# The down product of a SwiGLU network by seven block products in place of eight

## The chip, the cores and the metric

One core of a Trainium2 chip runs the whole encoder in one launch. The metric is device time in microseconds (us) of that launch. Five engines work side by side, each through its own instructions in program order: PE (TensorE: matmuls and transposes), ACT (ScalarE), DVE (VectorE), POOL (GpSimd) and SP, which only issues DMAs here. They wait for each other on semaphores.

## The reference, cut to what matters

256 tokens of width 1024 go through two layers. Each layer is: half an FFN, a token mixer, half an FFN. So there are four FFNs, all of this kind:

```python
def swiglu(h, w_gu, w_down):
    g, u = jnp.split(h @ w_gu, 2, axis=-1)
    return (jax.nn.silu(g) * u) @ w_down
# x = x + 0.5 * rms_norm(swiglu(rms_norm(x, g_pre), w_gu, w_down), g_post)
# h: 256 x 1024, w_gu: 1024 x 5632, w_down: 2816 x 1024, all float32
```

The first mixer is a retention layer, the second a latent attention. The change leaves both alone.

## The kernel before, in words

Every product of two float32 matrices is made of three matmuls in a rounded format: each operand is split into a high part (`h`, made by a cast on ACT) and a low part (`l`, the difference, made by a subtraction on DVE), and `mm3` (lines 135 to 138) adds high by high, high by low and low by high into one PSUM bank of 128 x 512. Weights go the same way: SP loads a raw tile, ACT casts it to `wh` (line 75), DVE subtracts to get `wl` (line 76). There are nine pairs of such weight tiles and five raw tiles, in rotation.

An FFN (`ffn`, from line 227) goes through 2816 inner columns in 11 chunks of 256. For chunk c and token half t (0 or 1), `gu(t, c)` makes the gate and up columns in one bank: 8 steps over the depth, 24 matmuls of 512 columns. `swiglu(t, c)` then reads the bank: a Silu on ACT (line 263), a multiplication on DVE (line 265), giving the activation `a`, and a block transpose on DVE (line 282) into `aT`. When two chunks and both halves are there, POOL and 12 small DMAs exchange blocks of `aT` into the tile `ag`, which holds the transposed activation (`turn`). `take(c)` splits it into `ah` and `al`; the table `landed` says behind which `swiglu` it is put: for an even chunk c behind `swiglu(0, c + 3)`, for an odd one behind `swiglu(1, c + 2)`. `both(c)` is the down product of a chunk: 2 token halves x 2 output halves x 2 depth blocks = 8 block products, 24 matmuls of 512 columns, summed over all chunks in four PSUM banks (`accs`). Four banks are left for gate and up.

PE's order is that of the Python code. In the main loop (c = 3 to 9) it is `gu(0, c)`, `gu(1, c)`, `both(c - 3)`. The order on ACT, DVE and SP is made by a scheduler when the kernel is built, from what is ready when in its own estimate and from edges such as `behind(s_ins, a_ins)`, which put one instruction behind another on the same engine. After that it is fixed. `post` scales a finished token half, adds it to `x` and prepares the next norm; the last call of it writes the output. The three Python functions at the end of the kernel (from line 1034) load `x` and the first weights and start the first FFN.

Of the kernel before, what the change touches and what calls it, by code (L numbers as in the profile page):

```python
# [18 lines left out]
P = 128  # L19
# [12 lines left out]
def kernel(ctx, tc, x, mem, positions, norm_gains, ffn_w_gu, ffn_w_down, w_o,  # L32
# [18 lines left out]
    def t2(name, n=512, dt=F32):  # L51
        return wk.tile([P, n], dt, name=name, tag="t2", bufs=8)
# [26 lines left out]
    def load_raw(src, cols):  # L79
        raw = raw_tile()  # L80
# [9 lines left out]
        return raw  # L90

    last_load = [None]

# [4 lines left out]
    ahead = []  # L98

# [43 lines left out]
    def rstd_of(halves, scale, eps, tag):  # L143
        ss = sm.tile([P, 2], F32, name="ss", tag="ss")
        for i, h in enumerate(halves):
            junk = wk.tile([P, 512], BF16, name="junk", tag="junk", bufs=1)
            S.activation(out=junk[:, :h.shape[1]], in_=h, func=AF.Square, scale=scale,  # L147
                         accum_out=ss[:, i:i + 1])
        ms = sm.tile([P, 1], F32, name="ms", tag="ms")
        if len(halves) == 2:  # L150
            V.scalar_tensor_tensor(out=ms, in0=ss[:, 0:1], scalar=eps, in1=ss[:, 1:2],
                                   op0=ALU.add, op1=ALU.add)
        else:
            V.tensor_scalar(out=ms, in0=ss[:, 0:1], scalar1=eps, scalar2=None, op0=ALU.add)
        r = sm.tile([P, 1], F32, name=tag, tag=tag)
        rsqrt(r, ms)
        return r
# [22 lines left out]
    def pre(t, gain):  # L180

        z = Z()
        parts = []
        for i in range(2):
            p = t2("z")
            V.tensor_tensor(out=p, in0=halves(xt[t])[i], in1=halves(gain)[i], op=ALU.mult)
            parts.append(p)

        def put_half(i):
            if i == 0:  # L190
                z.h, z.l = ztile()
# [5 lines left out]
        def put():  # L197
            put_half(0)
            with tc.issue_after(put_half(1)):
                rstd()  # L200
        z.put, z.put_half, z.rstd = put, put_half, rstd
        return z

    def post(t, accs, gain, half, next_gain, hook=None):
# [5 lines left out]
        ends = next_gain is None  # L210
        if not ends:
            scaled(0)
            scaled(1)
        r = rstd_of(accs, 1.0 / 16.0 if half else 1.0 / 32.0, (4.0 if half else 1.0) * EPS, "prs")
        if ends:
            scaled(0)
            scaled(1)
        for i in range(2):
            xx = halves(xt[t])[i]
            V.scalar_tensor_tensor(out=xx, in0=y[i], scalar=r, in1=xx, op0=ALU.mult, op1=ALU.add)  # L220
            if ends:
                nc.sync.dma_start(out=out[0, t * P:(t + 1) * P, i * 512:(i + 1) * 512], in_=xx)
            if hook and i == 0:
                hook()
        return None if next_gain is None else pre(t, next_gain)

# [5 lines left out]
    def ffn(l, j, zs, gains, extra=(), first=None):  # L232
        wgu, wd = ffn_w_gu[l, j], ffn_w_down[l, j]
        gu_w, d_w, act, at, pair = {}, {}, {}, {}, {}
        accs = [[None, None], [None, None]]
        extra = dict(extra)
# [7 lines left out]

        def gu(t, c, part=None):
            z = zs[t]
            if c not in gu_w:
                load_gu(c)
            if part != 1:
                act[t, c] = bank()  # L250
            p = act[t, c]
            for k in range(KB) if part is None else range(part * 4, part * 4 + 4):
                wh, wl = gu_w[c][k // 2]
                n = slice((k % 2) * 512, (k % 2 + 1) * 512)
                m = slice(k * P, (k + 1) * P)
                mm3(p, z.h[:, m], z.l[:, m], wh[:, n], wl[:, n], k == 0, k == KB - 1)
            if part is None:
                swiglu(t, c)

        def swiglu(t, c):  # L260
# [4 lines left out]
            a_ins = V.scalar_tensor_tensor(out=a, in0=p[:, FC:2 * FC], scalar=z.r, in1=s,  # L265
                                           op0=ALU.mult, op1=ALU.mult).ins
            if (t, c) == (1, NFC - 1) or first and (t, c) == (0, 0):
                ahead[:] = [s_ins, a_ins]
            act[t, c] = a
            if c < C:  # L270
                turn(t, c)
            for k in [k for k in list(pair) if landed(k) == (t, c)]:
                with behind(s_ins, a_ins):
                    take(k)

        def turn(t, c):
# [7 lines left out]
            if t == 1 and c % 2:  # L284
                g = wk.tile([P, 1024], F32, name="ag", tag="ag", bufs=1)
                for i in range(4):
                    sl = slice(i * 32, (i + 1) * 32)
                    G.tensor_copy(out=g[sl, i * 256:(i + 1) * 256], in_=b[sl, i * 256:(i + 1) * 256])  # L288
                    for q in range(4):
                        if q != i:  # L290
                            nc.sync.dma_start(out=g[q * 32:(q + 1) * 32, i * 256:(i + 1) * 256],  # L291
                                              in_=b[sl, q * 256:(q + 1) * 256])
                pair[c - 1], pair[c] = g, g
# [5 lines left out]
        def take(c):  # L299
            g = pair.pop(c)  # L300
# [14 lines left out]
        def down(t, c, hs=(0, 1)):  # L315
# [3 lines left out]
            for i in hs:  # L319
                if c == 0:  # L320
                    accs[t][i] = bank()
                for b in range(2):
# [4 lines left out]
                        c == 0 and b == 0, c == NFC - 1 and b == 1)  # L327

        def both(c):
            down(0, c)  # L330
            down(1, c)

        if first:
            gu_w[0] = first
            gu(0, 0, 0)
            zs[1].put()
            gu(0, 0, 1)
            swiglu(0, 0)
            gu(1, 0)
            gu(0, 1)  # L340
        else:
            gu(0, 0)
            gu(0, 1, 0)
# [4 lines left out]
        gu(1, 1)  # L348
        gu(0, 2)
        gu(1, 2)  # L350
        for c in range(3, C):
            gu(0, c)
            gu(1, c)
# [6 lines left out]
            both(c - 3)  # L360
# [8 lines left out]
        with in_order():  # L369
            z0 = post(0, accs[0], gain_post, True, next_gain, lambda: swiglu(1, C))  # L370
# [4 lines left out]
        if z0:  # L375
            z0.put()
        down(1, C, (1,))
        z1 = post(1, accs[1], gain_post, True, next_gain)
# [267 lines left out]
    def retention(zs, mkv, gains):  # L646
# [204 lines left out]
        z1 = post(1, W.accs[1], gain_post, False, next_gain)  # L851
        return [z0, z1]


    def mla(zs, mkv, gains):
# [173 lines left out]
        z1 = post(1, W.accs[1], gain_post, False, next_gain)  # L1029
        return [z0, z1]  # L1030
# [8 lines left out]
    g0 = wk.tile([P, DM], F32, name="gpre", tag="gpre", bufs=1)  # L1039
    grow = g0[0:1, 512:1024]  # L1040
    ones = k1("ones", P)[0:1, :]
    V.memset(ones, 1.0)
    nc.scalar.dma_start(out=grow, in_=norm_gains[0, 0, 512:1024].unsqueeze(0))
    load_x(0, 0)
    bcast(g0[:, 0:512], norm_gains[0, 0, 0:512])
    load_x(0, 1)
    first = [load_raw(gu_src(ffn_w_gu[0, 0], 0, u), 1024) for u in range(2)]
    for i in range(2):
        load_x(1, i)
    first += [load_raw(gu_src(ffn_w_gu[0, 0], 0, u), 1024) for u in range(2, 4)]  # L1050
# [10 lines left out]

    def warm(n):
        w = bank()
        for i in range(n):
            T.transpose(out=w[:, (i % 4) * P:(i % 4 + 1) * P], in_=ident, identity=ident)
    warm(8)
    g0 = [g0[:, 0:512], bank()]
    T.matmul(out=g0[1], lhsT=ones, rhs=grow, start=True, stop=True)
    with in_order():
        zs = [pre(0, g0)]  # L1070
        first[0] = split_raw(first[0], 1024, (lambda: zs[0].put_half(0), lambda: (warm(3), zs[0].put_half(1))))
        first[1] = split_raw(first[1], 1024, (lambda: None,) * 2)
        zs.append(pre(1, g0))
    zs[0].rstd()
    first[2:] = [split_raw(r, 1024) for r in first[2:]]
# [14 lines left out]
    def mem_extra(m):  # L1090
# [9 lines left out]
        return {6: first, 7: second, 8: third}  # L1100

    m0 = Mem(0)
    zs = ffn(0, 0, zs, lambda: (gpost(0, 1), gpre(0, 2)), {3: tables, 4: tables2, **mem_extra(m0)}, first=first)
    zs = retention(zs, m0, lambda: (gpost(0, 3), gpre(0, 4)))
    zs = ffn(0, 1, zs, lambda: (gpost(0, 5), gpre(1, 0)))
    m1 = Mem(1)
    zs = ffn(1, 0, zs, lambda: (gpost(1, 1), gpre(1, 2)), mem_extra(m1))
    zs = mla(zs, m1, lambda: (gpost(1, 3), gpre(1, 4)))
    ffn(1, 1, zs, lambda: (gpost(1, 5), None))
# [34 lines left out]
```

## Time and profile before

| what | value |
|---|---|
| device time, median of 3 runs (lowest, highest) | 964.87 us (963.84, 966.45) |
| the profiled execution's own time | 965.5 us |
| span of its trace, first to last instruction | 963.7 us |
| PE busy | 949.9 us, 99% |
| DVE busy | 626.2 us, 65% |
| ACT busy | 516.2 us, 54% |
| mean granted TensorE clock | 0.999 |

1.8 us of the profiled execution's time lie around the span. A busy PE is not a PE without slack: a matmul's record is longer than the step from one to the next, since they are pipelined, so the step has to be read from the start times. The idle time of ACT and DVE costs nothing as long as PE finds its operands.

### The profile page before, as it was taken

Reading aid. Unit: us, or ns where it says so; the run is one execution under the profiler, and the core shown is the slowest. Engines: PE = TensorE matmul, PEld = TensorE weight load, DVE = VectorE, ACT = ScalarE, POOL = GpSimd, SP = SyncE. Lnnn points to the kernel's source line nnn. Section 1 sums busy time; section 2 is a strip of 40 time slices with the busy share of each in tenths; the row PEclk is TensorE's granted clock in tenths of the full one; section 3 lists DMA queues with packets and bytes.
Section 4 is the critical chain, followed back from the end, with each engine's and each line's share of the span. In section 5 each row is a group of like instructions: output and inputs, shape, how many; then the busy total and the mean of one; then the engine's idle time right before and its main releaser. Section 6 shows DMA issues by size and latency. Waiting matters only on the chain.

```text
span 963.7 us, 13202 instructions
## 1 busy us (share of the span) xinstructions
PE 949.9 (99%) x4503; PEld 789.2 (82%) x4503; DVE 626.2 (65%) x989; ACT 516.2 (54%) x859; POOL 87.5 (9%) x122
## 2 busy tenths in 40 slices
PE   8999999999999999999999999999999999999997
PEld 6887888898878888888887888888897888888886
DVE  6766567586886775655558656655666886566552
ACT  6535456465665654544446444555568864444441
POOL 0110111010000111101101111101010011111010
PEclk9999999999999999999999999999999999999999
DMA  8668677493645556867546676875561746777631
GB/s 276 213 221 274 208 226 249 133 313 103 208 156 162 153 149 234 288 209 211 173 127 204 217 243 223 260 240 165 155 204 32 231 125 198 238 238 225 221 104 44
DMA packets 148679, 189.23 MB, mean 196 GB/s; under 512 B 13314, under 2 KB 130818, under 8 KB 148611
## 3 DMA queue, kind: packets, MB, share of 16 engines
q1 hardware_dynamic: 148608, 188.38, 61.2%
q8 instruction: 35, 0.57, 0.2%
q14 instruction: 34, 0.27, 0.1%
q10 hardware_dynamic: 2, 0.00, 0.0%
HBM read 179.42 MB, written 1.05 MB: 187 GB/s over the span
## 4 chain that ended last, share of the span: by engine, by line
PE 81%; DMA 7%; DVE 4%; ACT 3%; issue 3%; SPq 2%; POOL 0%; DVEq 0%; POOLq 0%; ACTq 0%
PE bank L138 26%; PE bank L136 26%; PE bank L137 26%; DMA raw<-in_ffn_w_gu_dram 4%; PE bank L162 2%; DVE wl L76 2%; ACT wh L75 2%; SPq L291 1%; DMA raw<-in_ret_w_in_dram 1%; DMA raw<-in_ffn_w_down_dram 1%; PE bank L493 1%; SPq L87 1%; ACT e L504 0%; DMA gpre<-in_norm_gains_dram 0%; DVE x L220 0%
## 5 line engine op out<-in xcount | busy, mean ns | idle before, releaser
L76 DVE TENSOR_TENSOR wl<-raw,wh 128x1024 fp32r<-128x1024 f32 (+2 forms) x326 | 388.6, 1209 | 164.6 <-ACT wh L75 158.2
L75 ACT CAST wh<-raw 128x1024 fp32r<-128x1024 f32 (+2 forms) x326 | 334.7, 1042 | 216.5 <-PE bank L138 78.4
L136 PE MATMUL bank<-wh,zh 128*128 128x512 f32 (+2 forms) x944 | 364.5, 386 | 0.6 <-ACT zh L75 0.4
L137 PE MATMUL bank<-wl,zh 128*128 128x512 f32 (+2 forms) x944 | 360.4, 382 | 0.6 <-DVE wl L76 0.6
L138 PE MATMUL bank<-wh,zl 128*128 128x512 f32 (+2 forms) x944 | 360.5, 382 | 0.4 <-DVE zl L76 0.4
L138 PEld LDWEIGHTS bank<-wh,zl 128*128 128x128 f32 x944 | 177.4, 188 | 35.4 <-DVE zl L76 1.4
L136 PEld LDWEIGHTS bank<-wh,zh 128*128 128x128 f32 x944 | 177.6, 188 | 34.8 <-ACT zh L75 0.9
L137 PEld LDWEIGHTS bank<-wl,zh 128*128 128x128 f32 x944 | 177.6, 188 | 34.5 <-DVE wl L76 1.6
L136 PE MATMUL bank<-wh,ah 128*128 128x512 f32 x352 | 138.0, 392 | 0.0
L138 PE MATMUL bank<-wh,al 128*128 128x512 f32 x352 | 137.4, 390 | 0.6 <-DVE al L76 0.6
L137 PE MATMUL bank<-wl,ah 128*128 128x512 f32 x352 | 137.0, 389 | 0.0
L288 POOL COPY ag<-aT 32x256 f32<-32x256 f32 x80 | 55.9, 699 | 481.6 <-DMA raw<-in_ffn_w_gu_dram 290.2
L263 ACT ACTIVATE s<-bank,rstd 128x256 f32<-128x256 f32 x88 | 41.5, 472 | 101.0 <-PE bank L138 100.9
L265 DVE SCALAR_TENSOR_TENSOR a<-bank,rstd,s 128x256 f32<-128x256 f32 x88 | 42.3, 480 | 59.5 <-ACT s L263 59.3
L138 PEld LDWEIGHTS bank<-wh,al 128*128 128x128 f32 x352 | 66.1, 188 | 15.2 <-DVE al L76 1.5
L137 PEld LDWEIGHTS bank<-wl,ah 128*128 128x128 f32 x352 | 66.1, 188 | 13.4
L136 PEld LDWEIGHTS bank<-wh,ah 128*128 128x128 f32 x352 | 66.1, 188 | 13.4 <-ACT ah L75 0.2
L147 ACT ACTIVATE junk<-bank 128x512 bf16<-128x512 f32 x24 | 14.3, 594 | 41.8 <-DVE y L209 29.4
L282 DVE STREAM_TRANSPOSE aT<-a 128x256 f32<-128x256 f32 x80 | 35.4, 443 | 1.5
L75 ACT CAST zh<-bank 128x512 fp32r<-128x512 f32 (+2 forms) x58 | 25.3, 462 | 19.4 <-PE bank L162 12.4
L76 DVE TENSOR_TENSOR zl<-bank,zh 128x512 fp32r<-128x512 f32 (+2 forms) x58 | 28.7, 519 | 6.0 <-ACT zh L75 6.0
L76 DVE TENSOR_TENSOR al<-ag,ah 128x256 fp32r<-128x256 f32 x80 | 31.3, 404 | 1.0 <-ACT ah L75 0.8
(154 smaller groups left out, 519.6 us busy)
## 6 DMA issues: line engine op xcount, KB each, us to landing
raw<-in_ffn_w_gu_dram SPq DMA_DIRECT2D x352, 256.0 KB, 4.7
raw<-in_ffn_w_down_dram SPq DMA_DIRECT2D x88, 512.0 KB, 5.4
raw<-in_ret_w_in_dram SPq DMA_DIRECT2D x48, 256.0 KB, 4.7
raw<-in_w_o_dram SPq DMA_DIRECT2D x16, 512.0 KB, 4.3
ag<-aT SPq DMA_DIRECT2D x240, 32.0 KB, 1.9
raw<-in_mem_w_kv_dram SPq DMA_DIRECT2D x8, 512.0 KB, 5.4
gpost<-in_norm_gains_dram SPq DMA_DIRECT2D x6, 512.0 KB, 6.2
gpre<-in_norm_gains_dram SPq DMA_DIRECT2D x5, 512.0 KB, 7.6
```

Of the source, the lines that this page charges most:

```text
L75: ins = S.copy(out=hi, in_=src).ins
L76: V.tensor_tensor(out=lo, in0=src, in1=hi.bitcast(F32), op=ALU.subtract)
L87: last_load[0] = nc.sync.dma_start(out=dst[:, k], in_=src[:, k]).ins
L136: T.matmul(out=dst, lhsT=ah, rhs=bh, start=start, stop=False)
L137: T.matmul(out=dst, lhsT=ah, rhs=bl, start=False, stop=False)
L138: T.matmul(out=dst, lhsT=al, rhs=bh, start=False, stop=stop)
L147: S.activation(out=junk[:, :h.shape[1]], in_=h, func=AF.Square, scale=scale, accum_out=ss[:, i:i + 1])
L162: T.transpose(out=tp[:s.shape[1], j * P:(j + 1) * P], in_=s, identity=ident)
L263: s_ins = S.activation(out=s, in_=p[:, 0:FC], func=AF.Silu, scale=z.r).ins
L265: a_ins = V.scalar_tensor_tensor(out=a, in0=p[:, FC:2 * FC], scalar=z.r, in1=s, op0=ALU.mult, op1=ALU.mult).ins
L282: V.transpose(out=b.rearrange("p (q u t b x) -> p u t q b x", q=4, u=2, t=2, b=2)[:, c % 2, t], in_=act.pop((t, c)).rearrange("p (b q x) - ...
L288: G.tensor_copy(out=g[sl, i * 256:(i + 1) * 256], in_=b[sl, i * 256:(i + 1) * 256])
```

## The change

In each FFN the down product of the first chunks (5 in the first and third FFN, 8 in the second and fourth; `fast`) is made by Strassen's scheme in its form with 15 additions. Token halves and depth blocks make a 2 x 2 block matrix of the activation, depth blocks and output halves one of the weights. Seven block products of 3 matmuls each (`down_fast`, 21 matmuls) take the place of eight. Their operands are sums and differences of blocks, made on DVE before the split: four of 128 columns for the activation (`take_fast`, tile `sr`), and three instructions of 1024, 512 and 512 columns for the weights (`load_fast`, tiles `wB` and `wB21`). The split parts get larger too: 3584 columns of weight in place of 2048 for a chunk, 896 of activation in place of 512.

The seven products are summed over the chunks in seven banks, and one bank is left for gate and up. So `swiglu` in these chunks copies the up half out of the bank on ACT before DVE multiplies. PE's order in the loop becomes `gu(0, c)`, 11 matmuls of `down_fast(c - 3)`, `gu(1, c)`, the other 10. `combine` adds the products up once, behind the last fast chunk, and the remaining chunks go on in four banks as before; `post` adds both sums.

Further edits come with it. The exchange into `ag` is cut into pieces of 2 (once 6) DMAs, each issued between two weight loads on SP. The take stands ahead of the transposes in `swiglu`. The first chunk of the first FFN is started by a class `First` that goes through the depth in 8 steps for both token halves. The tables and the memory loads move to other chunks, the square sum of `z0` at an FFN's end moves behind `post` of the other half, and the last output goes out in more pieces.

```diff
+        def load_fast(c):
+            w = wk.tile([P, 1536], F32, name="wB", tag="A", bufs=2)
+            w21 = esm("wB21")
+            with behind(*moved):
+                last_load[0] = nc.sync.dma_start(out=w[:, 0:1024], in_=block(c, 0, 0, 2)).ins
+            loaded()
+            with behind(*moved):
+                nc.sync.dma_start(out=w[:, 1024:1536], in_=block(c, 1, 1))
+                last_load[0] = nc.sync.dma_start(out=w21, in_=block(c, 1, 0)).ins
+            loaded()
...
+            split(three[:, 0:3:2], two(xh), two(xl))
+            V.tensor_tensor(out=w[:, 0:1024], in0=w[:, 512:1536], in1=w[:, 0:1024], op=ALU.subtract)
+            split(w[:, 0:1024], yh, yl)
+            split(w21, vh[:, lo], vl[:, lo])
+            V.tensor_tensor(out=three[:, 2], in0=three[:, 2], in1=three[:, 0], op=ALU.subtract)
+            split(three[:, 2], th, tl)
+            V.tensor_tensor(out=w21, in0=w21, in1=three[:, 2], op=ALU.subtract)
+            split(w21, vh[:, hi], vl[:, hi])
...
+        def take_fast(c):
...
+            V.tensor_tensor(out=q(sr, 0), in0=A[1][0], in1=A[1][1], op=ALU.add)
+            V.tensor_tensor(out=q(sr, 1), in0=q(sr, 0), in1=A[0][0], op=ALU.subtract)
+            V.tensor_tensor(out=q(sr, 2), in0=A[0][0], in1=A[1][0], op=ALU.subtract)
+            V.tensor_tensor(out=q(sr, 3), in0=A[0][1], in1=q(sr, 1), op=ALU.subtract)
...
+            split(A[1][1], q(ah, 2), q(al, 2))
+            split(sr, sh, sl)
...
+            at[c] = [a(0), z(3), z(0), z(2), a(1), a(2), z(1)]
+        def down_fast(c, *ms):
...
+            for m in ms:
+                p, x = divmod(m, 3)
+                (ah, al), (bh, bl) = at[c][p], d_w[c][p]
+                own = p in (1, 4, 5)
+                T.matmul(out=prod[p], lhsT=al if x == 2 else ah, rhs=bl if x == 1 else bh,
+                         start=c == 0 and x == 0, stop=x == 2 and c == fast - 1 and not own)
...
+            if 3 <= c < fast + 3 and (t, c) != (1, C):
+                u = k1("u")
+                s_ins = S.activation(out=u, in_=p[:, FC:2 * FC], func=AF.Copy, scale=z.r).ins
+                a_ins = V.tensor_tensor(out=a, in0=u, in1=s, op=ALU.mult).ins
...
-            if c < C:
-                turn(t, c)
             for k in [k for k in list(pair) if landed(k) == (t, c)]:
                 with behind(s_ins, a_ins):
                     take(k)
+            if c < C:
+                turn(t, c)
...
         for c in range(3, C):
             gu(0, c)
+            if c - 3 < fast:
+                down_fast(c - 3, *range(11))
             gu(1, c)
...
-            both(c - 3)
+            if c - 3 < fast:
+                down_fast(c - 3, *range(11, 21))
+                if c - 3 == fast - 1:
+                    combine()
+            else:
+                both(c - 3)
```

What this does to the order of the instructions is shown at three places. The first is PE in the second FFN, chunk 5. Names: `zh` and `zl` are the normed input, `ah`, `al`, `sh`, `sl` the split activation and its sums for chunk 2; `bank_3912` in the kernel before is the gate and up bank of token half 1. Before:

```order
L138 MATMUL bank_3876<-wh_3872,zl_3205 128x512
L136 MATMUL bank_3912<-wh_3851,zh_3354 128x512
...
L138 MATMUL bank_3912<-wh_3872,zl_3355 128x512
L136 MATMUL bank_3691<-wh_3967,ah_3906 128x512
L137 MATMUL bank_3691<-wl_3968,ah_3906 128x512
L138 MATMUL bank_3691<-wh_3967,al_3907 128x512
```

The same place now, with `bank_4086` and `bank_4170` as the gate and up banks of the two halves:

```order
L159 MATMUL bank_4086<-wh_4082,zl_3364 128x512
L367 MATMUL bank_3822<-wh_4138,ah_4117 128x512
L367 MATMUL bank_3822<-wl_4139,ah_4117 128x512
L367 MATMUL bank_3822<-wh_4138,al_4118 128x512
L367 MATMUL bank_3823<-wh_4138,sh_4120 128x512
L367 MATMUL bank_3823<-wl_4139,sh_4120 128x512
L367 MATMUL bank_3823<-wh_4138,sl_4121 128x512
L367 MATMUL bank_3824<-wh_4140,sh_4120 128x512
...
L367 MATMUL bank_3825<-wl_4141,sh_4120 128x512
L157 MATMUL bank_4170<-wh_4055,zh_3513 128x512
```

The 24 matmuls of token half 1 stood between the end of `gu(0, 5)` and the first matmul that reads `ah`. Now that matmul is the next one. The second place is ACT there now, from the Silu of `gu(0, 5)` (`s_4111`) on; `wB` and `wB21` are raw down weights, `raw` raw gate and up weights of the next chunk:

```order
L402 ACTIVATE s_4111<-bank_4086,rstd_3386 128x256
L406 ACTIVATE u_4114<-bank_4086,rstd_3386 128x256
L75 CAST wh_4140<-wB_4133 128x1024
L75 CAST ah_4117<-ag_3887 128x256
L75 CAST ah_4117<-ag_3887 128x128
L75 CAST wh_4142<-wB21_4134 128x512
L75 CAST wh_4235<-raw_4232 128x1024
L75 CAST sh_4120<-sr_4119 128x512
```

Before, the Silu was followed by the two casts to `ah` at once. The third place is DVE now in the chunk after it (6), from the last instructions ahead of the multiplication `a_4287` of `gu(0, 6)` on; `wl_4305` is the low part of the second group of down weights, which products 2 and 3 read:

```order
L76 TENSOR_TENSOR sl_4205<-sr_4203,sh_4204 128x512
L76 TENSOR_TENSOR wl_4303<-wB_4293,wh_4302 128x1024
L407 TENSOR_TENSOR a_4287<-u_4288,s_4285 128x256
L322 TENSOR_TENSOR wB_4293<-wB_4293 128x1024
L426 STREAM_TRANSPOSE aT_4291<-a_4287 128x4x64
L325 TENSOR_TENSOR wB_4293<-wB_4293 128x512
L76 TENSOR_TENSOR wl_4305<-wB_4293,wh_4304 128x1024
```

The difference of weights (line 322) and the low part made from it stand behind the multiplication that waits for `gu(0, 6)`. The kernel before had no such difference.

## Rows read from the trace of the kernel before

**Rows 1.** The page, sections 1 and 2: busy time of each engine, granted TensorE clock
```profile
PE 949.9 (99%) x4503; PEld 789.2 (82%) x4503; DVE 626.2 (65%) x989; ACT 516.2 (54%) x859; POOL 87.5 (9%) x122
...
PEclk9999999999999999999999999999999999999999
```

**Rows 2.** Waits of PE: waited for, us in total, times, longest
```profile
PE bank L162 <- DVE z L186: 2.5, 2, 1.3
PE bank L525 <- ACT pT L516: 1.4, 2, 0.9
```

**Rows 3.** Groups of PE by form: xcount, busy us, mean ns, idle before
```profile
L136 PE MATMUL bank<-wh,zh 128*128 128x512 f32 x864 | 340.7, 394 | 0.6 <-ACT zh L75 0.4
L136 PE MATMUL bank<-wh,ah 128*128 128x512 f32 x352 | 138.0, 392 | 0.0
```

**Rows 4.** Timeline of PE in the third FFN: start, duration, engine, line
```profile
649.03 0.39 PE L138 MATMUL bank<-wh,zl 128*128 128x512 f32 x1
649.26 0.39 PE L136 MATMUL bank<-wh,zh 128*128 128x512 f32 x1
...
654.48 0.39 PE L138 MATMUL bank<-wh,zl 128*128 128x512 f32 x1
654.70 0.39 PE L136 MATMUL bank<-wh,ah 128*128 128x512 f32 x1
```

**Rows 5.** Timeline of ACT in the same stretch
```profile
649.46 0.47 ACT L263 ACTIVATE s<-bank,rstd 128x256 f32<-128x256 f32 x1 [4.12 <-PE bank L138]
649.83 0.70 ACT L75 CAST ah<-ag 128x256 fp32r<-128x256 f32 x2
```

**Rows 6.** Timeline of DVE in the same stretch
```profile
649.97 0.48 DVE L265 SCALAR_TENSOR_TENSOR a<-bank,rstd,s 128x256 f32<-128x256 f32 x1 [2.34 <-ACT s L263]
650.37 0.42 DVE L76 TENSOR_TENSOR al<-ag,ah 128x256 fp32r<-128x256 f32 x1
650.70 0.44 DVE L282 STREAM_TRANSPOSE aT<-a 128x256 f32<-128x256 f32 x1
651.06 0.39 DVE L76 TENSOR_TENSOR al<-ag,ah 128x256 fp32r<-128x256 f32 x1
```

**Rows 7.** Groups of ACT by form: casts of 1024, 512 and 128 columns
```profile
L75 ACT CAST wh<-raw 128x1024 fp32r<-128x1024 f32 x314 | 326.4, 1054 | 211.9 <-PE bank L138 76.8 <-DMA raw<-in_ffn_w_gu_dram 58.4 <-DMA raw<-in_ffn_w_down_dram 48.6
...
L75 ACT CAST zh<-bank 128x128 fp32r<-128x128 f32 x20 | 5.7, 287 | 6.9 <-PE bank L525 4.2 <-DVE zl L76 2.7
...
L75 ACT CAST wh<-raw 128x512 fp32r<-128x512 f32 x4 | 2.3, 622 | 0.0
```

**Rows 8.** Groups of DVE by form: 1024 and 512 columns, and small ones
```profile
L76 DVE TENSOR_TENSOR wl<-raw,wh 128x1024 fp32r<-128x1024 f32 x314 | 379.2, 1224 | 162.9 <-ACT wh L75 156.5
...
L76 DVE TENSOR_TENSOR wl<-raw,wh 128x512 fp32r<-128x512 f32 x4 | 2.6, 683 | 0.0
...
L640 DVE TENSOR_TENSOR qs<-qs,krt 128x96 f32<-128x96 f32 x4 | 1.0, 257 | 0.0
```

**Rows 9.** The page, DMA issues: count, KB each, median us from issue to landing
```profile
raw<-in_ffn_w_gu_dram SPq DMA_DIRECT2D x352, 256.0 KB, 4.7
raw<-in_ffn_w_down_dram SPq DMA_DIRECT2D x88, 512.0 KB, 5.4
...
ag<-aT SPq DMA_DIRECT2D x240, 32.0 KB, 1.9
```

**Rows 10.** Timeline of PE at the start: first gate-and-up product to the third
```profile
9.00 0.72 PE L136 MATMUL bank<-wh,zh 128*128 128x512 f32 x1
...
22.98 0.39 PE L136 MATMUL bank<-wh,zh 128*128 128x512 f32 x1
```

**Rows 11.** Timeline of the end: last matmul and last scaling
```profile
957.24 0.39 PE L138 MATMUL bank<-wh,al 128*128 128x512 f32 x1
...
958.52 0.69 DVE L209 TENSOR_TENSOR y<-bank,gpost 128x512 f32<-128x512 f32 x1
```

More of the change, by code (lines that the diff above doesn't have):

```diff
@@ L98, with norm_behind @@
     ahead = []
+    behind_post = []
+    def norm_behind(z):
+        if z:
+            with behind(*behind_post):
+                z.rstd()
     def behind(*inss):
@@ L195, in rstd, with put, post @@
             z.r = rstd_of(halves(xt[t]), 1.0 / 32.0, EPS, "rstd")
-        def put():
+        def put(norm=True):
             put_half(0)
-            with tc.issue_after(put_half(1)):
-                rstd()
+            last = put_half(1)
+            if norm:
+                with tc.issue_after(last):
+                    rstd()
         z.put, z.put_half, z.rstd = put, put_half, rstd
         return z
-    def post(t, accs, gain, half, next_gain, hook=None):
+    def post(t, accs, gain, half, next_gain, hook=None, sums=(None, None)):
         y = [t2("y") for i in range(2)]
@@ L210, in post @@
         ends = next_gain is None
+        if sums[0] is not None:
+            for a, b in zip(accs, sums):
+                V.tensor_tensor(out=b, in0=a, in1=b, op=ALU.add)
+            accs = sums
         if not ends:
@@ L230, in gu_src, with ffn @@
                 .rearrange("(k p) (h f) -> p k h f", p=P, h=2)[:, :, :, c * FC:(c + 1) * FC])
-    def ffn(l, j, zs, gains, extra=(), first=None):
+    def ffn(l, j, zs, gains, extra=(), first=None, fast=0):
         wgu, wd = ffn_w_gu[l, j], ffn_w_down[l, j]
@@ new lines, in down_fast @@
+        def down_fast(c, *ms):
+            if c not in d_w:
+                load_fast(c)
+            if c == 0 and 0 in ms:
+                prod.extend(bank() for _ in range(7))
+                accs[0][:] = prod[4], prod[1]
+                accs[1][0] = prod[5]
+            for m in ms:
[4 more added lines that the diff above has]
+                         start=c == 0 and x == 0, stop=x == 2 and c == fast - 1 and not own)
@@ L245, in gu, with combine @@
+        def combine():
+            m1, m5, m7, m6 = prod[0], prod[2], prod[3], prod[6]
+            c1, u, v, w = esm("c1"), esm("u"), esm("v"), esm("w")
+            S.copy(out=c1, in_=m1)
+            add = lambda o, a, b: V.tensor_tensor(out=o, in0=a, in1=b, op=ALU.add)
+            add(u, m6, c1)
+            add(v, m5, u)
+            add(u, m7, u)
+            add(w, m5, u)
+            sums[:] = [[c1, v], [u, w]]
         def gu(t, c, part=None):
-            z = zs[t]
             if c not in gu_w:
@@ L285, in turn @@
                 g = wk.tile([P, 1024], F32, name="ag", tag="ag", bufs=1)
[L286 to L292, printed above, removed]
+                skip, n = (6, 6) if c == 1 else (4, 2) if c < C - 1 else (0, 12)
+                exchange(b, g, skip, n)
                 pair[c - 1], pair[c] = g, g
@@ L299, in take @@
         def take(c):
+            assert not between, between
+            if c < fast:
+                return take_fast(c)
             g = pair.pop(c)
@@ L333, in ffn @@
         if first:
[L334 to L339, printed above, removed]
+            gu_w[0] = first.w
+            first.run(lambda t, k: gu_k(t, 0, k))
+            load_gu(1)
+            for t in range(2):
+                first.rstd(t)
+                swiglu(t, 0)
             gu(0, 1)
@@ L1059, in gpost @@
         return gain_tile(norm_gains[l, j], "gpost")
+    wbank = bank()
     def warm(n):
-        w = bank()
         for i in range(n):
-            T.transpose(out=w[:, (i % 4) * P:(i % 4 + 1) * P], in_=ident, identity=ident)
+            T.transpose(out=wbank[:, (i % 4) * P:(i % 4 + 1) * P], in_=ident, identity=ident)
     warm(8)
[L1067 to L1073, printed above, removed]
```

232 lines of the change are left out of this document (187 added, 45 removed).

## The prediction

> **What bounds the kernel now.** I read the page first: PE is busy 99% of the span, DVE 65%, ACT 54%, and the granted clock is at its upper level (2.4 GHz) in all 40 slices [rows 1]. Then the waits of PE alone: the largest are 2.5 and 1.4 us in all [rows 2]. So nearly nothing is gained by making another engine faster, and nearly everything that makes PE wait shows in the time. Next, what a matmul costs. Its record is about 390 ns long [rows 3], but the timeline of PE shows 24 of them from 649.26 to 654.70 us [rows 4]: 5.44 / 24 = 0.227 us from one to the next. That step, not the 390 ns, is what a removed matmul gives back. Last, the same place on ACT and DVE, since it shows how long the answer to a gate and up product takes: the last matmul of it starts at 649.03, the Silu at 649.46, the next ACT instruction at 649.83; DVE multiplies from 649.97 to 650.45 [rows 4 to 6]. PE reads the new `ah` only at 654.70, since 24 other matmuls lie between. This is the cover that hides the answer now.
>
> **What is removed.** Three matmuls in each of 5 + 8 + 5 + 8 = 26 chunks: 78 x 0.227 = 17.7 us. The weight load of each is inside the step. Nothing on PE is added.
>
> **What is added on DVE and ACT.** For a chunk, DVE splits 1536 more weight columns (1.5 x 1.22 = 1.8 us), makes differences of 1024, 512 and 512 columns (1.22 + 2 x 0.68 = 2.6), four sums of 128 columns (no row of that size; 0.26 by the row of 96 columns; bounds 0.15 and 0.42, the latter for 256 columns; so 1.0) and splits 384 more columns of activation (0.4) [rows 6, 8]. Together 5.8 us. Before, 65% of the 16.3 us of a chunk (72 matmuls x 0.227) is 10.6 us, so now 16.4 us, against 69 x 0.227 = 15.7 us of PE. Even if nobody ever waited, DVE could not deliver the chunk in PE's time. ACT gets 1.6 us more of casts and two copies and stays below.
>
> **The wait at even chunks.** The loop now puts the first 11 matmuls of the down product straight behind `gu(0, c)`. The take of an even chunk is still placed behind `swiglu(0, c)` of that same product, on ACT as on DVE. So PE waits for an answer that it has only just made possible. I walk along the order shown for chunk 5, with time 0 at the start of the last gate and up matmul. ACT: Silu at 0.43, copy at 0.80, both done at 1.27 (the copy taken as long as the Silu); then in its order a cast of 1024 (done at 2.2), `ah` (0.35 and 0.29, done at 2.9), 512 (3.5), 1024 (4.5), `sh` 512 (5.15) [rows 5, 7]. DVE: the multiplication from 1.27 (0.40 to the next), three sums (2.45), transposes (0.36), the fourth sum (3.1), a low part of 1024 (4.3), `al` (0.33 and 0.26, 4.9), a low part of 512 (5.6), `sl` (6.2) [rows 6, 8]. PE's sixth matmul of the block reads `sl`. It could have started at 6 x 0.227 = 1.36, so it is 4.9 us late, and with it all that is queued behind it on PE: five more matmuls, `gu(1, c)`, the rest. ACT and DVE go on with weights in that time, so the later parts of the block find theirs. For chunk 0 of an FFN the order has one long instruction less on each engine: 4.2 us. For chunks 4 and 6 the second group of weights is made earlier: 3.7 us. There are 4 chunks 0, 4 chunks 2, 4 chunks 4 and 2 chunks 6: 4 x 4.2 + 4 x 4.9 + 6 x 3.7 = 58.6 us. Bounds: if nothing foreign stood between, the chain copy, multiplication, four sums, cast `sh`, `sl` would end at 1.27 + 0.40 + 1.04 + 0.62 + 0.68 = 4.0, 2.7 us late, 38 us for 14 chunks; with one more 1024-column instruction ahead of each (1.22), 76 us.
>
> **The wait at odd chunks.** Their take stands behind `swiglu(1, c)` a chunk earlier and has 34 matmuls of cover. But on DVE the difference of weights that products 2 and 3 need stands behind the multiplication of `gu(0, c)`. From time 0 again: multiplication done at 1.67, difference 1.22 (2.9), its cast on ACT 1.05 (3.9), its low part 1.22 (5.2) [rows 6 to 8]. PE's eighth matmul reads it and was due at 1.82: 3.3 us. Besides, SP has the second load of these weights behind the first piece of the exchange, which waits for the transposes of `gu(1, c)`. These end about 3.7 us behind its last matmul (copy, multiplication, four sums, `al`, transposes), and `gu(0)` of the next chunk ends 34 x 0.227 = 7.7 us behind it. The first cast of the chunk (1.05) needs that load and stands ahead of the Silu, so the load has 7.7 + 0.43 - 1.05 - 3.7 = 3.4 us to land unnoticed. It has 256 KB; loads of 32 KB land in 1.9 us, of 512 KB in 5.4 [rows 9]. So 0 to 2.0 us; I take 1.0. That is 4.3 us at 10 chunks (1 and 3 in the short ones, 1, 3 and 5 in the long ones; chunk 7's order has the difference ahead): 43 us, with bounds 33 and 53.
>
> **The rest.** At the start, the two halves of chunk 0 take PE from 9.00 to 22.98 us [rows 10], where 48 matmuls need 10.9; in 8 steps for both halves at once some of the 3 us of gaps go. A gain of 0 to 5 us, I take 3. At the end one addition of 512 columns from PSUM comes between the last matmul and the square: 0.69 by the scaling of that form [rows 11]; inside, three FFN ends cost 0 to 1.4 each, I take 0, since the other token half's matmuls cover them. `combine` gives DVE 4 x 0.69 us per FFN, 0 to 2.8; I take 0, hidden by the weights made ahead. The one bank for gate and up must be read within 10 or 11 matmuls (2.3 to 2.5 us) and is free at 1.27: no cost, up to 0.4 us if a 1024-column cast stands ahead. Moved tables and memory loads: PE does not wait for them before and has more time now; nothing.
>
> **The sum**, against the profiled execution: 965.5 - 17.7 + 58.6 + 43 - 3 + 0.7 = 1047 us; the median of the runs is 0.6 lower, so 1046. With the bounds of the two waits and of the start: 965 - 17.7 + 38 + 33 - 5 = 1013 and 965 - 17.7 + 76 + 53 + 3 = 1079.
>
> **Rivals.** *Only the bare chain counts.* The order of ACT and DVE is fixed, but if both run ahead during the waits, the odd chunks lose nothing and the even ones the 2.7 us: 965 - 17.7 + 38 - 3 = 982. For it speaks that DVE is idle a third of the time now; against it, that the difference stands behind the multiplication in every odd chunk named. 0.12.
>
> *PE's clock falls in the waits.* The trace shows no waits of this length in the stream of matmuls and the upper level throughout, so it cannot tell. If the granted clock fell to 1.2 GHz for the 11 matmuls behind each of the 24 waits, each would take a step twice as long: 24 x 11 x 0.227 = 60 us more, 1106. 0.10. The Trainium skill says, in "TensorE: Matmul & The Clock Gate" under "HAM oscillation", that pauses for other work between bursts of matmuls put the clock back and that each burst then starts slow. By that rule the time would be near this rival's; the trace neither agrees nor differs.
>
> *Faster, or the same.* If PE found its operands after all, because the answer takes less than the walk says, DVE would set the pace at about 16.4 us per chunk or somewhat below, against 16.3 before: between nothing and the whole 17.7 us, so 946 to 963, say 955. It decides at a wait of 2 x 3 x 0.227 = 1.36 us per pair of chunks: below that the change gains. For it speaks that this kernel hides such answers everywhere (the largest sums of waits are 2.5 and 1.4 us [rows 2]); against it, that the first read of `ah` follows its own product directly, and that Silu and copy alone put it 1.27 us behind. 0.09.
>
> **How the numbers follow.** The forecast has 0.69, the others 0.12, 0.10 and 0.09. A measurement of this kernel can tell a difference of 0.3% (2.9 us) from none. Of the last rival 0.07 is faster and 0.02 the same; 0.01 of the first is the same too. So faster 0.07, same 0.03, slower 0.90. The range goes from 990, between the bare chain and the lower bound, to 1090, between the upper bound and the clock rival's time; that leaves out about 0.2.
>
> **What would show it.** PE's waits by name: in the timeline of a chunk with even number a gap of 2 us or more behind the last gate and up matmul, ended by the cast to `ah`, and one ended by `sl`; in odd chunks one ended by the cast and low part of the difference of weights. PE's busy time lower by some 18 us and its idle time higher by 100. A pair of fast chunks should take about 39 to 40 us in place of 32.7. I am wrong if these gaps stay under 1 us, if DVE is busy 95% in these stretches with PE waiting for gate and up weights, or if the granted clock falls.

## The result, and the profile after

The changed kernel takes 1086.52 us (median of 4 runs, 1082.06 to 1087.57) against 964.91 (963.84 to 966.45): a ratio of 1.125 [1.123, 1.127]. It is slower, as forecast, and 40 us above the predicted 1046. It lies inside the stated range of 990 to 1090, but above 1079, where the sum of the waits ends with all its upper bounds. The profiled execution took 1087.57 us with a span of 1085.8, so 1.8 us lie around the span, as before.

The page after, sections 1 and 2, against [rows 1]:

```profile
PE 990.6 (91%) x4425; PEld 796.4 (73%) x4425; DVE 785.2 (72%) x1318; ACT 590.1 (54%) x1031; POOL 80.8 (7%) x122
...
PEclk9988899999999989988999898999999998989999
```

There are 78 matmuls fewer (4503 to 4425), yet PE's busy time rose by 41 us, and the granted clock is no longer at 9 in all slices; its mean is 0.953 (1.0 is the upper level, 2.4 GHz, and 0.5 the lower, 1.2 GHz). So part of the new time is idle PE, part is slower PE. The waits of PE, where [rows 2] had nothing above 2.5 us (waited for: us in total, times, longest):

```profile
PE bank L367 <- ACT ah L75: 46.4, 14, 7.2
PE bank L367 <- ACT wh L75: 18.8, 20, 1.5
PE bank L367 <- DVE wl L76: 14.6, 20, 0.8
PE bank L367 <- DVE al L76: 3.0, 6, 0.8
...
PE bank L367 <- DVE sl L76: 0.9, 3, 0.3
```

All lie in the first 11 matmuls of a fast chunk (line 367): 14 waits for `ah`, at the even chunks, and 20 each for `wh` and `wl`, two of each at the 10 odd chunks.

An even chunk, the place that the prediction walked along (second FFN, `gu(0, 5)` and the down product of chunk 2), in the timeline of all engines (start, duration, engine, line):

```profile
435.51 0.39 PE L159 MATMUL bank<-wh,zl 128*128 128x512 f32 x1
435.94 0.47 ACT L402 ACTIVATE s<-bank,rstd 128x256 f32<-128x256 f32 x1 [1.05 <-PE bank L159]
436.18 1.22 DVE L322 TENSOR_TENSOR wB<-wB 128x1024 f32<-128x1024 f32 x1
436.31 0.47 ACT L406 ACTIVATE u<-bank,rstd 128x256 f32<-128x256 f32 x1
437.32 0.42 DVE L407 TENSOR_TENSOR a<-u,s 128x256 f32<-128x256 f32 x1
437.44 1.04 ACT L75 CAST wh<-wB 128x1024 fp32r<-128x1024 f32 x1 [0.66 <-DVE wB L322]
...
438.39 0.60 ACT L75 CAST ah<-ag 128x256 fp32r<-128x256 f32 x2
...
438.84 0.50 PE L367 MATMUL bank<-wh,ah 128*128 128x512 f32 x1 [2.94 <-ACT ah L75]
...
440.40 0.80 PE L367 MATMUL bank<-wh,al 128*128 128x512 f32 x1 [0.82 <-DVE al L76]
...
441.03 0.80 PE L367 MATMUL bank<-wh,sh 128*128 128x512 f32 x1
441.07 0.68 DVE L76 TENSOR_TENSOR sl<-sr,sh 128x512 fp32r<-128x512 f32 x1
441.63 0.63 PE L367 MATMUL bank<-wl,sh 128*128 128x512 f32 x1
...
442.05 0.63 PE L367 MATMUL bank<-wh,sl 128*128 128x512 f32 x1
```

Time 0 is 435.51. The Silu comes at 0.43 as in [rows 5], the multiplication at 1.8, the cast to `ah` at 2.9, and the sixth matmul, which reads `sl`, at 6.5; the walk said 0.43, 1.3, 2.2, 6.2. The multiplication is late because DVE is in a difference of weights (line 322) from 436.18. After the first gap the matmuls also step differently: 441.63 to 442.05 is 0.42 us, where [rows 4] have 0.227. That is 1.85 times as long, and the granted clock there is 0.50, the 1.2 GHz level, in the last of these windows (us of the window, busy time of PE, PEld, DVE, ACT and POOL, granted clock, DMA share, GB/s):

```profile
436.00:439.00 3.00, 0.16 (x1) 0.16 (x2) 2.97 (x9) 2.34 (x6) 0.00 (x0) 1.00 1.02 346
439.00:442.00 3.00, 2.18 (x5) 1.13 (x6) 3.00 (x6) 2.93 (x4) 0.00 (x0) 0.72 0.21 83
442.00:446.00 4.00, 4.00 (x15) 3.24 (x15) 3.73 (x5) 2.29 (x4) 0.00 (x0) 0.78 0.02 4
446.00:450.00 4.00, 4.00 (x19) 3.30 (x19) 3.06 (x4) 0.97 (x2) 0.00 (x0) 1.00 0.00 0
441.00:443.00 2.00, 2.00 (x6) 1.51 (x6) 2.00 (x4) 1.17 (x2) 0.00 (x0) 0.50 0.04 8
```

The clock falls behind the gap of 2.94 us and is back at the upper level in the window from 446, with PE busy in between. DVE was done with `sl` at 441.75, 6.2 us from time 0 as the walk said; the slow step put its read 0.3 us behind that. The clock did not fall everywhere: by the trace's record of it, in or behind 18 of the 24 blocks, and of the four blocks whose only gap was 2.17 us behind two.

The odd chunk after it (`gu(0, 6)`, down product of chunk 3), same view:

```profile
457.13 1.05 ACT L75 CAST wh<-wB 128x1024 fp32r<-128x1024 f32 x1 [4.15 <-DMA wB<-in_ffn_w_down_dram]
457.16 0.39 PE L159 MATMUL bank<-wh,zl 128*128 128x512 f32 x1
...
459.35 0.42 DVE L407 TENSOR_TENSOR a<-u,s 128x256 f32<-128x256 f32 x1
...
459.69 1.22 DVE L322 TENSOR_TENSOR wB<-wB 128x1024 f32<-128x1024 f32 x1
...
460.94 1.57 ACT L75 CAST wh<-wB 128x1024 fp32r<-128x1024 f32 x2 [2.02 <-DVE wB L322]
...
462.01 1.82 DVE L76 TENSOR_TENSOR wl<-wB,wh 128x1024 fp32r<-128x1024 f32 x2 [0.18 <-ACT wh L75]
462.03 0.49 PE L367 MATMUL bank<-wh,sh 128*128 128x512 f32 x1 [1.10 <-ACT wh L75]
...
463.29 0.50 PE L367 MATMUL bank<-wl,sh 128*128 128x512 f32 x1 [0.77 <-DVE wl L76]
```

Cast late for its load, multiplication, difference (line 322), its cast, its low part, PE: the chain of the prediction, in its order. The eighth matmul comes at 463.29, due at 457.16 + 8 x 0.227 = 458.98, so 4.3 us late, as forecast. Why the load is late stands on SP (DMA queue):

```profile
435.49 0.55 SPq L309 DMA_DIRECT2D wB<-in_ffn_w_down_dram  x1
453.02 1.21 SPq L267 DMA_DIRECT2D ag<-aT  x2
454.27 0.58 SPq L312 DMA_DIRECT2D wB<-in_ffn_w_down_dram  x1
```

SP issues nothing from 436.0 to 453.0: the first piece of the exchange waits for the transpose of `gu(1, 5)`, and the second load of chunk 3's weights, with all loads behind it, waits in line. The sum of these waits in SP's queue:

```profile
SPq L267 <- DVE aT L426: 222.3, 18, 21.6
```

**Where the 122 us lie.** I added up, over all matmuls of 512 columns, what each step has above 0.227 us, apart for steps at a wait and steps without one. At waits: 4.4 us before, 100.2 after, so +95.8. Without a wait: 6.8 before, 52.4 after, so +45.6; steps at a granted clock below 1 have 42 us of it. The first such matmul starts at 6.42 in place of 9.00 [rows 10], -2.6:

```profile
6.42 0.67 PE L157 MATMUL bank<-wh,zh 128*128 128x512 f32 x1
```

The last one starts 7.5 us ahead of the span's end in place of 6.5 [rows 11], +1.1:

```profile
1078.26 0.39 PE L159 MATMUL bank<-wh,al 128*128 128x512 f32 x1
```

With the removed matmuls, -17.7, that makes 95.8 + 45.6 - 2.6 + 1.1 - 17.7 = 122.2, and the span grew by 1085.8 - 963.7 = 122.1.

### The profile page after: what moved, and what is told of

The parts are those of the page before. It is cut to its first block, busy times and chain, and to the rows that moved or that the text cites. A ratio compares the mean times of both kernels' runs of the same rounds, so it can differ in the third digit from the quotient of the medians.

```text
span 1085.8 us, 13518 instructions
## 1 busy us (share of the span) xinstructions
PE 990.6 (91%) x4425; PEld 796.4 (73%) x4425; DVE 785.2 (72%) x1318; ACT 590.1 (54%) x1031; POOL 80.8 (7%) x122
## 4 chain that ended last, share of the span: by engine, by line
PE 61%; DMA 11%; DVE 10%; SPq 10%; ACT 5%; issue 3%; POOL 0%; DVEq 0%; POOLq 0%; ACTq 0%
PE bank L157 16%; PE bank L158 16%; PE bank L159 16%; PE bank L367 7%; DMA raw<-in_ffn_w_gu_dram 5%; SPq L267 4%; SPq L91 3%; DVE wl L76 3%; DMA wB<-in_ffn_w_down_dram 3%; PE bank L187 2%; ACT wh L75 2%; DMA raw<-in_mem_norm_dram 1%; DMA raw<-in_ret_w_in_dram 1%; DVE a L407 1%; DVE al L76 1%
## 5 line engine op out<-in xcount | busy, mean ns | idle before, releaser
L76 DVE TENSOR_TENSOR wl<-raw,wh 128x1024 fp32r<-128x1024 f32 (+1 forms) x268 | 318.1, 1211 | 61.0 <-ACT wh L75 59.1
L75 ACT CAST wh<-raw 128x1024 fp32r<-128x1024 f32 (+1 forms) x268 | 275.4, 1045 | 121.8 <-DMA raw<-in_ffn_w_gu_dram 42.0
L76 DVE TENSOR_TENSOR wl<-wB,wh 128x1024 fp32r<-128x1024 f32 (+1 forms) x104 | 98.2, 957 | 76.8 <-ACT wh L75 76.2
L75 ACT CAST wh<-wB 128x1024 fp32r<-128x1024 f32 (+1 forms) x104 | 85.1, 833 | 121.3 <-DMA wB<-in_ffn_w_down_dram 69.7
L367 PE MATMUL bank<-wh,ah 128*128 128x512 f32 x78 | 35.4, 454 | 54.4 <-ACT ah L75 46.4
L367 PEld LDWEIGHTS bank<-wh,ah 128*128 128x128 f32 x78 | 15.3, 197 | 66.7 <-ACT ah L75 52.3
L157 PE MATMUL bank<-wh,ah 128*128 128x512 f32 x144 | 57.1, 396 | 0.0
L159 PE MATMUL bank<-wh,al 128*128 128x512 f32 x144 | 56.2, 390 | 0.0
L158 PE MATMUL bank<-wl,ah 128*128 128x512 f32 x144 | 56.1, 390 | 0.0
L367 PE MATMUL bank<-wh,sh 128*128 128x512 f32 x78 | 41.2, 528 | 10.9 <-ACT wh L75 10.8
L367 PE MATMUL bank<-wl,sh 128*128 128x512 f32 x78 | 40.5, 519 | 7.0 <-DVE wl L76 7.0
L367 PE MATMUL bank<-wl,ah 128*128 128x512 f32 x78 | 33.6, 431 | 7.6 <-DVE wl L76 7.6
```

What stands on the lines that cost most here:

```text
L75: ins = S.copy(out=hi, in_=src).ins
L76: V.tensor_tensor(out=lo, in0=src, in1=hi.bitcast(F32), op=ALU.subtract)
L157: T.matmul(out=dst, lhsT=ah, rhs=bh, start=start, stop=False)
L158: T.matmul(out=dst, lhsT=ah, rhs=bl, start=False, stop=False)
L159: T.matmul(out=dst, lhsT=al, rhs=bh, start=False, stop=stop)
L367: T.matmul(out=prod[p], lhsT=al if x == 2 else ah, rhs=bl if x == 1 else bh, start=c == 0 and x == 0, stop=x == 2 and c == fast - 1 and no ...
```

## The experiments

Theory A is the prediction's: PE waits for operands that the order places too late, `ah` and the sums at even chunks, the loads and the difference at odd ones. Rivals: E, DVE or ACT has not the time for the added work, whatever the order; C, the clock; B, other edits cost time by themselves. All change the changed kernel, but for the eighth, which changes the kernel before. Each ran beside the kernel before (medians of 964.9 to 965.3).

**1. Without the scheme**, all other edits kept.

```diff
-    zs = ffn(0, 1, zs, lambda: (gpost(0, 5), gpre(1, 0)), fast=8)
+    zs = ffn(0, 1, zs, lambda: (gpost(0, 5), gpre(1, 0)), fast=0)
```

(and so in all four calls)

> All four FFNs with fast = 0: the down products by eight block products in four banks as before, everything else of the change kept (start by class First, cut exchange, moved tables and loads). Theory A (the slowdown comes from the two waits at the down blocks of fast chunks and from the clock that falls in them): the waits are gone, granted clock above 0.99, time = 965 minus the gain at the start (5 us by the trace of the changed kernel), 957 to 963 us. Rival B (the other edits cost, above all the exchange cut into pieces, which makes SP wait): 970 us or more even without a fast chunk.

984.24 us (983.74 to 988.54), ratio 1.021 [1.018, 1.023]. B is right: the other edits cost some 19 us with no Strassen product at all. Its waits on PE and SP:

```profile
PE bank L158 <- DVE wl L76: 8.9, 15, 0.8
PE bank L157 <- ACT wh L75: 6.5, 5, 3.7
```

```profile
SPq L267 <- DVE aT L426: 120.3, 17, 9.7
```

PE now waits for gate and up weights, whose loads stand behind pieces of the exchange on SP.

**2. Zero matmuls in the waits**, so that PE is not idle there: 13 to 17 (9 in later chunks) ahead of the block and a few inside it at even chunks, 4 or 5 at four places at odd ones.

```diff
...
+            gaps = {} if c == 7 else {0: 4, 1: 4, 6: 5, 7: 4} if c % 2 else even
             for m in ms:
+                for i in range(gaps.get(m, 0)):
+                    T.matmul(out=prod[6][0:112], lhsT=zero, rhs=gu_w[c + 3][i % 4][0][:, 0:512], ...)
```

> The changed kernel, with matmuls of a zero tile put into the waits on PE (9 to 17 ahead of the first matmul of an even block, 2 to 5 ahead of the later matmuls that waited; they add zero to a product bank). They are to fill idle time, so they leave the operands as late as they are. Theory C (the 46 us of slower steps come from PE's granted clock falling because PE idles): clock above 0.99, steps of 0.227 us throughout, time 1086 - 46 = 1036 to 1048 us. Rival D (the steps are slower for another reason, such as DVE and ACT reading the same memory): clock and steps as in the changed kernel, 1080 to 1095 us.

1078.98 us (1078.49 to 1079.96), ratio 1.118 [1.117, 1.120]. The granted clock is 0.996, and still only 7.5 us came back, so neither case holds as written. Measured from the last gate and up matmul to the first one behind the 11, the blocks are together 133 us late with the filling as without: at some chunks it ran on past the arrival of the operand (down chunk 4 of the second FFN: 6.4 us late in place of 4.0). The price of the clock was not told by this run.

**3. The exchange in one piece.**

```diff
-                skip, n = (6, 6) if c == 1 else (4, 2) if c < C - 1 else (0, 12)
+                skip, n = 0, 12
```

> One line: the exchange into ag is issued in one piece of 12 DMAs, as before the change, everything else as in the changed kernel. By the order of the built kernel, DVE then has the difference of the weights (line 322) ahead of the multiplication in odd chunks too, and in even chunks the casts to ah and sh stand straight behind the copy. Theory A: no wait is left at odd chunks (they held 49 us of lateness), at even chunks the bare chain, about 2.9 us each at 14 chunks, 41 us; 965 - 18 - 5 + 41 = 983, with some clock loss 983 to 1000 us. Rival E (the odd chunks wait because DVE as a whole is too slow, not because of the place of that instruction): the odd waits stay, above 1030 us.

997.56 us (996.43 to 999.18), ratio 1.033 [1.032, 1.035]. A is right, E falls. This one line is worth 89 us of the 122. No odd chunk is late any more (0.00 at all ten); the even ones are late by 52.9 us together, where 41 were expected. What is left in PE's waits:

```profile
PE bank L367 <- ACT ah L75: 19.4, 14, 3.5
```

The load is early at odd chunks, and the order on DVE has turned too: the difference now stands ahead of the multiplication (an odd chunk in this kernel's timeline of DVE).

```profile
402.83 1.22 DVE L322 TENSOR_TENSOR wB<-wB 128x1024 f32<-128x1024 f32 x1
404.09 0.69 DVE L325 TENSOR_TENSOR wB<-wB 128x512 f32<-128x512 f32 x1
404.70 0.42 DVE L407 TENSOR_TENSOR a<-u,s 128x256 f32<-128x256 f32 x1
```

**4. The even take half a chunk earlier as well**: the uncut exchange of 3, and the take behind `swiglu(1, c + 2)`.

```diff
-            return (0, min(c + 3, C)) if c % 2 == 0 else ...
+            return ((1, c + 2) if c < fast else (0, min(c + 3, C))) if c % 2 == 0 else ...
```

> The uncut exchange, and besides the take of an even fast chunk c behind swiglu(1, c + 2) in place of swiglu(0, c + 3), so that 10 matmuls of the block before and 24 of gate and up lie between it and its first reader. Theory A: no wait is left at even chunks either; clock above 0.99. Then either PE sets the pace, 965 - 18 - 5 = 942 to 948 us, or DVE, whose work per fast chunk I put at 16.4 us against 16.3 of the chunk before: 955 to 965 us, with PE waiting for low parts of weights spread over the fast chunks. Rival E (latency does not matter, DVE's amount of work does): above 975 us.

946.98 us (946.36 to 948.04), ratio 0.981 [0.980, 0.983]: faster than both kernels, and the theory that PE sets the pace holds. All blocks together are 3.0 us late.

```profile
PE 931.5 (98%) x4425; PEld 775.5 (82%) x4425; DVE 787.6 (83%) x1318; ACT 589.6 (62%) x1031; POOL 105.8 (11%) x122
...
PEclk9999999999999999999999999999999999999999
```

Two windows of the second FFN show DVE's load, first in the kernel before, then in this one:

```profile
400.00:480.00 80.00, 80.00 (x355) 66.24 (x354) 46.47 (x59) 37.75 (x51) 7.37 (x12) 1.00 0.63 198
```

```profile
390.00:470.00 80.00, 80.00 (x354) 66.27 (x353) 76.35 (x118) 52.72 (x81) 9.73 (x12) 1.00 0.68 220
```

DVE is busy 95% here, 0.954 x 69 x 0.227 = 14.9 us per chunk, just under PE's 15.7.

**5. Without the scheme, exchange in one piece**: the edits of 1 and 3 together.

> No fast chunk (as in the run without Strassen's scheme, 984.2 us) and the exchange uncut. Theory F (the cut exchange by itself makes SP issue weight loads late and cost that run its 19 us over the kernel before): 957 to 963 us, the kernel before less the 5 us gained at the start; against the uncut kernel with early takes (947.0) the scheme itself would then give 12 to 16 of its 17.7 us. Rival G (another edit cost the 19 us: moved tables and memory loads, the later square sum): 975 us or more.

963.15 us (959.8 to 966.84), ratio 0.998 [0.996, 0.999]. So the cut exchange costs 984.24 - 963.15 = 21 us without the scheme. The other edits together gave 1.8 us, with 3.7 us gained at the start (the 49th matmul of 512 columns begins at 19.32 for 22.98); what else they cost was not separated. And the scheme by itself gives 963.15 - 946.98 = 16.2 us when its operands are early, of the 17.7 counted.

**6. Less filling**: 16 zero matmuls at chunk 0, 11 and 3 at chunk 2, 8 at other even chunks, 3 or 4 at four places at odd ones.

> The changed kernel with fewer zero matmuls in the waits (3 to 16 in place of 4 to 17, and none where a wait had gone), so that they hardly push what comes behind them. Theory C (granted clock falls because PE idles, and that costs net time): clock above 0.98 and 1050 to 1070 us. Theory H (the clock does fall because of the idling, but matmuls that run slowly inside a wait cost nothing, since they would wait for operands anyway, so that its net price is small): clock above 0.98 and 1070 to 1080 us.

1070.83 us (1068.96 to 1070.9), ratio 1.109 [1.108, 1.111], clock 0.994. It lies at the edge between the two cases. With the clock held the time falls by 15.7 us, so the clock's net price is about 16 us or more. What became of the other 30 of the 45.6 us isn't separated: slow steps where the next operand was late anyway, and filling that still ran too long at some places. An estimate can be had from the trace of the changed kernel: if every operand comes when it does there and every other step takes 0.227 us, the 24 blocks end 18 us earlier in all, and the slow steps at the lower clock behind them are 12 more, so about 30 us.

**7. The block behind both halves**: `gu(0, c)`, `gu(1, c)`, then all 21, with the cut exchange.

```diff
-            if c - 3 < fast:
-                down_fast(c - 3, *range(11))
             gu(1, c)
...
-                down_fast(c - 3, *range(11, 21))
+                down_fast(c - 3, *range(21))
```

> The changed kernel, exchange cut as there, but PE's order in the loop is gate and up of both halves, then all 21 matmuls of the down block. Theory A (what waits is the block that stands directly behind its own answer): the waits for ah, sl and the low parts go; in their place gu(1, c) waits for the single bank to be read, 1.27 us less a step, 1.1 us at 24 chunks, 27 us. With the 19 us that the cut exchange cost without any fast chunk: 965 - 18 - 5 + 27 + 0 to 19 = 970 to 990 us, clock above 0.99. Rival E (DVE is too slow for the scheme's extra work): above 1020 us.

1058.21 us (1056.17 to 1059.6), ratio 1.097 [1.095, 1.098]: A's number missed by some 70 us, and E's (above 1020) fits. The waits for `ah` are gone but for one (1.8 us), and others stand in their place:

```profile
PE bank L157 <- ACT u L406: 22.8, 20, 3.1
PE bank L367 <- DVE wl L76: 19.9, 22, 2.6
PE bank L367 <- ACT wh L75: 12.6, 10, 2.9
```

The first is the single gate and up bank, 1.1 us each time as expected. The other two are low and high parts of down weights, as if the cover of PE's order did nothing for them. E would explain that as well as late loads would; the ninth run decides.

**8. The kernel before with PE's interleaved order**, to see whether the order costs without the scheme.

```diff
             gu(0, c)
+            down(0, c - 3)
             gu(1, c)
...
-            both(c - 3)
+            down(1, c - 3)
```

> The kernel before, with PE's order alone changed in the manner of the change: gate and up of half 0, down product of half 0, gate and up of half 1, down product of half 1; eight block products, four banks, whole exchange. Theory A: at the 16 even chunks the down product waits for the take behind its own Silu: ah at about 1.2 us (first matmul due at 0.23), al at 1.8 (third due at 0.68), so 1.1 us late each, 18 us: 978 to 988 us, clock above 0.99. Rival (four free banks let PE go on and nothing is lost): 962 to 968 us.

1001.65 us (1000.26 to 1004.39), ratio 1.039 [1.036, 1.041]. The mechanism is A's, its size was taken too low by some 14 us.

```profile
PE bank L136 <- ACT ah L75: 19.8, 16, 4.1
```

So the order alone, with no difference, sum or product of the scheme, loses 37 us.

**9. Block behind both halves, exchange in one piece**: the edits of 7 and 3 together, to settle the miss of 7.

> PE's order is gu(0, c), gu(1, c), then all 21 matmuls, and the exchange of aT is in one piece. Theory A: the low parts that were late with the same order of PE came from the weight loads behind the pieces of the exchange. Then with the exchange in one piece only the wait for the single gate and up bank is left, about 1.1 us at each of 24 chunks: 965 - 18 - 5 + 26 = 968 us, 962 to 978, and PE's waits for wh and wl at the down products (20 and 13 us with the exchange in pieces) fall below 5 us together. Rival R: ACT and DVE are late by their own order, since the weights of the block are made ahead by too little whatever SP does. Then those waits stay above 15 us and the time is above 1000 us.

974.0 us (973.41 to 974.75), ratio 1.009 [1.007, 1.012]. A is right, R falls. The bank's wait is the only one of size left:

```profile
PE bank L157 <- ACT u L406: 20.2, 20, 2.4
```

So the late weights of 7 came with the cut exchange, and not from too much work on DVE or ACT; E falls there too.

## Why the prediction was right, and where not

**Direction and mechanism: right, and shown.** The gaps stand where the prediction put them and are ended by what it named, the cast to `ah` at all 14 even blocks, cast and low part of weights at all 10 odd ones; only `sl` ended few (3, 0.9 us in all), since elsewhere the matmuls ahead of it, slow ones among them, filled the time until it came. Both causes were taken away one by one: with the exchange in one piece (3) the odd waits went, with the earlier take (4) the even ones, and then the scheme gained. Experiment 8 shows the even wait by itself: the order alone costs 37 us. A pair of fast chunks took 43.4 us (435.5 to 478.9 between two last gate and up matmuls ahead of even blocks), where 39 to 40 were forecast. PE's idle time rose by 81 us (100 forecast), and its busy time rose by 41, where a fall of 18 was forecast: its records are longer at the lower clock.

**The step that failed: the sum had no term for the clock.** It priced every matmul at the upper level and gave the fall a rival of 0.10; a falling clock was also the last of its signs of being wrong, and the mean fell to 0.953. What the sum added up is how late the sixth matmul of an even block and the eighth of an odd one start. Measured so, the even blocks are 71.5 us late in all (58.6 forecast) and the odd ones 44.5 (43): 116 for 101.6, slow steps inside them included. The other 25 of the 95.8 + 45.6 = 141.4 us are slow steps in the main and lie behind those matmuls, where the sum had nothing. With start and end 0.4 higher each: 14.4 + 25.4 + 0.8 = 40.6, and 1087.6 - 1047 is that. So the measured time lies in the range by its margin, not by its sum: the range had been opened beyond 1079 only towards the rival.

The rival "PE's clock falls in the waits" had the right mechanism, with 60 us where the trace has 46, at 18 of the 24 blocks. How much of the 46 would come back with a steady clock is measured from below only, by the 16 us of experiment 6; about 30 by the estimate there. The rule cited from the Trainium skill ("TensorE: Matmul & The Clock Gate", section "HAM oscillation") agrees with this trace at those 18 blocks: behind 2.94 us of idle PE the steps take 0.42 us, at a granted clock of 0.50. At the other six no fall followed the waits.

**Within the blocks, chunk 0 was off furthest.** Its sixth matmul is 9.5 us late in the first FFN and 6.1 to 6.3 in the others, where 4.2 were taken; that of chunk 2 4.5 to 5.4 (4.9 forecast), of chunks 4 and 6 3.3 to 5.6 (3.7). The eighth matmul of an odd block is 4.3 to 5.2 us late (4.3). For chunk 0 the prediction counted one long instruction less on each engine. In the trace DVE makes a low part and two differences of weights ahead of the multiplication (second FFN, time 0 at 391.77):

```profile
392.28 1.23 DVE L76 TENSOR_TENSOR wl<-wB,wh 128x1024 fp32r<-128x1024 f32 x1 [3.92 <-ACT wh L75]
393.54 1.22 DVE L322 TENSOR_TENSOR wB<-wB 128x1024 f32<-128x1024 f32 x1
...
395.41 0.42 DVE L407 TENSOR_TENSOR a<-u,s 128x256 f32<-128x256 f32 x1
...
396.20 0.79 PE L367 MATMUL bank<-wh,ah 128*128 128x512 f32 x1 [4.05 <-ACT ah L75]
```

In the first FFN ACT's first cast of the block waited for its load besides, until 48.60, 2.6 us behind time 0. Measured to the first matmul behind the 11, with slow steps among them, even blocks are 84.2 us late in all and odd ones 48.7.

**The two parts of the odd term go away together.** The prediction gave 3.3 us to the order on DVE and 1.0 to the load behind the cut exchange, as two things. Inside the block shown that split holds: the multiplication starts 2.2 us from time 0, where 1.3 were walked without a late load. But both go away with the one line of experiment 3, which also turned the order on DVE; probably the scheduler, expecting the load late, had put the difference late (that was not tested apart). That SP's queue would stand still for 17 us at a time, and that the cut exchange would cost 21 us even without the scheme (1 against 5), was not foreseen.

**DVE's load was taken from the wrong stretch.** The forecast used the mean of the span, 65% of 16.3 us, and got 16.4 us per chunk, above PE's 15.7. The stage itself has 46.47 of 80 us, 58%: 9.5 + 5.8 = 15.3, and 14.9 was measured. So the faster rival ("DVE would set the pace", 955) was priced too high in time: with early operands PE sets the pace at 947.

**Small terms.** Removed: 17.7 counted, 16.2 measured (5 against 4). Start: PE's first product began 2.6 us earlier and took 1.5 us less (its 49th matmul begins at 18.86 for 22.98 [rows 10]), together 4.1; 3 us were forecast within 0 to 5. The upper sum of 1079 has +3 where the start's own bound allows 0 at most: 1076 by its own terms. End: +1.1, forecast +0.7. The four sums of 128 columns took 0.28 each, taken as 0.26. The single bank cost nothing in the interleaved order, as forecast; in the order of 7 and 9 it costs 20 to 23 us.

## What to carry to other kernels

A scheme that saves matmuls pays only if its operands are ready earlier, not just on average in time: look for the first matmul that reads the answer to the product directly ahead of it, and move the work that feeds it, here by half a chunk, before counting the gain. A DMA that waits for computed data held every load behind it in SP's queue here (17 us in the chunk shown), so cutting it into pieces between loads can cost more than the piece saves. And a wait of PE can have a second price behind it, slower matmuls (here 46 us of slow steps, of which 16 at least counted), so a sum of waits alone can come out too low; take each engine's load from the stage at hand, not from the span.

## What the runs showed of the hardware

- The granted clock fell to 0.50 behind an idle stretch of PE of 2.94 us, with steps of 0.42 us, and was at the upper level again in the window from 446 us, after matmuls without a gap. It fell so in or behind 18 of 24 blocks with waits, six odd ones among them, whose longest gap was 1.1 us. Matmuls on zeros in the gaps kept its mean at 0.996 (2).
- Restoring the clock from 0.953 to 0.996 in that way gave 7.5 us of 1086.5, and with less filling 15.7 at 0.994: a higher granted clock is not by itself a shorter time.
